# Query halves placed by DMA, feed-forward sums formed during the mixer, weights held over two halves, and low halves moved from GpSimd to VectorE

## The chip, the cores and the metric

The kernel runs on one core of a Trainium2 chip. The metric is the device time of one execution in microseconds (us), lower is better. The engines are TensorE (PE; its weight loads are PEld), VectorE (DVE), ScalarE (ACT), GpSimd (POOL) and SyncE (SP), which issues the DMAs.

## The reference

One step of a two-layer encoder over 1024 prompt frames and 32 sample frames, 1056 columns in all, width 1024. Layer A is an mLSTM mixer, layer B a sliding-window attention of 16 query heads on 2 key heads with sinks and a linear bias. Each has an output product, a residual with a layer norm, a SwiGLU feed-forward block of inner width 2816, and again a residual with a norm:

```python
def layer_norm(x, g, b):
    mu = jnp.mean(xf, -1, keepdims=True)
    var = jnp.mean(jnp.square(xf - mu), -1, keepdims=True)
    return (xf - mu) * lax.rsqrt(var + LN_EPS) * g + b

def swiglu(x, w_gu, w_down):
    g, u = jnp.split(x @ w_gu, 2, axis=-1)
    return (jax.nn.silu(g) * u) @ w_down

# every sub-layer: x = layer_norm(alpha * x + sublayer(x))
```

## The kernel before

**Layout.** x lies feature-major: 8 tiles of 128 features by 1056 columns, in `ACT` (float32) and in `SX` as a high and a low half. Columns are worked on in four quarters of 264 (two quarters are a half, `c`), in the attention in three groups of 384, 384 and 288.

**Products.** All matmuls keep float32 accuracy by splitting both operands: high is the operand rounded to the matmul type, low is the rest. `gemm` (L360 to L362) issues three matmuls per pair of tiles: high by high, high by low, low by high. So each operand needs a cast on ScalarE (for weights L200, for norms L468, for sums L1277) and a subtraction for the low half (L202, L474, L1274) on VectorE or GpSimd.

**Weights.** `Weights` loads units of 512 KB from HBM by SyncE (`wr`, three buffers, L159) and splits each in two parts, up to five live. A unit in `on_vector` has its low half on VectorE, else on GpSimd. A unit that has a `home` is split into other memory: the eight units of a mixer's output product are partly kept in `E`, which later holds the feed-forward's sums.

**Order of work.** The instruction order of each engine is fixed when the program is built. The main program writes products; `gemm` gives the estimated TensorE time of each to `wv.tick`, and the weaver `wv` lets side tasks, written as generators, issue their next step when their `yield` time has passed. `wv.drain` runs a task to its end.

**Mixer output and norm.** `mixer_out` computes the output product quarter by quarter; VectorE adds each tile to the residual (L1135) and forms the column sums (L600, L602). `ln_task` then runs as a side task: TensorE averages over the features (L421), VectorE centres (L426), ScalarE squares, L430 adds the squares (partly on GpSimd), L433 is the last addition, TensorE averages (L437), VectorE scales (L452), ScalarE applies gain and bias, and the result is split (cast L468, low half L474, odd pairs on GpSimd). The mixers' norms have `li` 0 and 2, the feed-forwards' 1 and 3; norm and products overlap by a quarter or more.

**Feed-forward.** The first two pairs of units of the up product (`FIRST` = 2) are computed plainly, for both halves: `up_plain`, 16 products of 24 matmuls per layer, with ScalarE's SiLU and VectorE's product L1253. The rest uses a seven-product scheme, `up_tile`, which needs four sums of pieces of x, called t1 to t4. `sums(c)` forms them while `up_plain` runs: VectorE adds or subtracts (L1287 to L1293) into buffers in `Z`, ScalarE casts (L1277), and L1274 forms the low half, on VectorE and GpSimd in turn:

```python
todo = [(o, k) for k in range(0, H, 2) for o in ("t3", "t2", "t4")] + [("t1", k) for k in range(0, H, 2)]
...
                        (nc.vector if s & 1 else nc.gpsimd).tensor_sub(d[:, 1], bufs[s % 2], d[:, 0].bitcast(F32))
```

**Queries.** `q_group(j, g)` makes one group of query columns for two heads. The score product (L1669, L1670) needs the high half of one head beside its low half on the other 64 partitions, so two ScalarE (L1580, L1581) and two VectorE instructions (L1582, L1585) write crosswise from PSUM into `Q`. Keys are copied across partitions by SyncE's DMAs (L1547, L1548, L1551). `attention` is a pipeline of scores (L1675 adds bias and takes a maximum), exponentials (L1687, L1691, L1693), transposes (L1713), their split (L1716, L1717) and the values; `ast["ready"]` counts the query groups it may use. Four groups are made ahead of the first scores, the other 20 while it runs.

Of the kernel before, what the change touches and what calls it, by code (L numbers as in the profile page):

```python
# [9 lines left out]
F32 = mybir.dt.float32  # L10
# [6 lines left out]
P = 128  # L17
D = 1024
KT = D // P
# [14 lines left out]

FIRST, TAIL = 2, 4
ALPHA = float((2 * DEPTH) ** 0.25)
LN_EPS = 1e-5
# [203 lines left out]
def kernel(ctx: ExitStack, tc: tile.TileContext, A, O):  # L241
# [46 lines left out]
    def add_ffn(layer):  # L288
        up, dn = {}, []
        for c in range(2):  # L290
            for i in range(FIRST):
                up[i, c] = [add("gu", 2 * (layer * FT + i) + k) for k in range(2)]
        for i in range(FIRST, FT):
            up[i] = add_pair("gu", 2 * (layer * FT + i))
        for b in range(TAIL):
            dn.append([add_pair("dn", 4 * (layer * TAIL + b) + 2 * j) for j in range(2)])
        dn.append([add("dnt", KT * layer + m) for m in range(KT)])
        on_vector.update((u, 1) for u in dn[TAIL])
        on_vector.update((u, f) for i in range(FIRST) for c in range(2) for u in up[i, c] for f in range(2))
        U_UP.append(up)  # L300
        U_DN.append(dn)
# [100 lines left out]
    def ln_task(z_, lps, grp, li, last, final):  # L402
# [20 lines left out]
        for s in range(n + 2):  # L423
# [25 lines left out]
        for s in range(n + 3):  # L449
# [138 lines left out]
    def norm_tail(li, run, box, final=False):  # L588
# [3 lines left out]
        for g, (cols, (c, zs)) in enumerate(QUARTERS):  # L592
# [18 lines left out]
            last = g >= 3  # L611
            tasks.append(wv.launch(ln_task(box[0].z, box[0].lnps, QUARTERS[g], li, last, final)))
        return tasks

# [436 lines left out]
    class Mixer(ExitStack):  # L1051
# [3 lines left out]
        def __init__(self, closing, us):  # L1055
# [7 lines left out]
            self.lnps = self.enter_context(pool("lnps", PSUM, side="right"))  # L1063
            for i, u in enumerate(us):
                for f in range(2):
                    W.home[u, f] = [self.E[:, h, 2 * i + f, : D // 2] for h in range(2)]

    def scratch(i, n):
# [49 lines left out]
    def mixer_out(us, li, lx, opening=None, before=None):  # L1118
# [3 lines left out]
        def run(g, cols, after):  # L1122
            if before:
                before(g)

            order = [6, 7, *range(6)] if g == 3 and not opening else list(range(KT))
            for i, m in enumerate(order):
# [8 lines left out]
                if g == 3 or u not in us[1]:  # L1136
                    W.done(u)
                if box[0]:
                    after(order, i)
# [10 lines left out]
    def ffn(layer, li, tasks, lx, final):  # L1150
# [15 lines left out]

        def natural(k0, par):
            return lambda c: SX[:, :, k0 : k0 + H, (2 * c + par) * N4 : (2 * c + par + 1) * N4]

        def extra(i):  # L1170
            return lambda c: E[:, :, H * i : H * (i + 1), c * N4 : (c + 1) * N4]

        X = {"x11": natural(0, 0), "x21": natural(H, 0), "x22": natural(H, 1), "t1": natural(0, 1)}
        extras = ("t2", "t3", "t4")
        X.update((o, extra(i)) for i, o in enumerate(extras))

# [61 lines left out]
        def up_plain(i, c):  # L1238
# [3 lines left out]
            for u in (ug, uu):  # L1242
                for par in range(2):
# [3 lines left out]
                    gemm(ps, wcols(u), x)  # L1247
                    if par:
                        W.done(u)
                    if u == ug:  # L1250
                        nc.scalar.activation(t, ps, AF.Silu)
                    else:
                        nc.vector.tensor_mul(t, t, ps)  # L1253

        plain = [False, False]
        made = []

        def sums(c):


            def x(k, par):
                return ACT[:, k : k + 2, group(2 * c + par)]

            todo = [(o, k) for k in range(0, H, 2) for o in ("t3", "t2", "t4")] + [("t1", k) for k in range(0, H, 2)]
            bufs = [Z[:, i : i + 2, c, :] for i in (7, 9)]
            while (li - 1, 3) not in squared:
                yield 0.3

            def halve(s, low):
                if 0 <= s < len(todo):  # L1270
                    o, k = todo[s]
                    d = X[o](c)[:, :, k : k + 2, :]
                    if low:
                        (nc.vector if s & 1 else nc.gpsimd).tensor_sub(d[:, 1], bufs[s % 2], d[:, 0].bitcast(F32))  # L1274
                        made.append((c, o))
                    else:
                        nc.scalar.copy(d[:, 0], bufs[s % 2])  # L1277

            for s in range(len(todo) + 2):
                halve(s - 2, True)  # L1280
                if s < len(todo):
                    o, k = todo[s]
                    while o == "t1" and not plain[c]:
                        yield 0.3
                    t, before = bufs[s % 2], bufs[(s - 1) % 2]
                    if o == "t3":
                        nc.vector.tensor_sub(t, x(k + H, 1), x(k, 1))  # L1287
                    elif o == "t2":
                        nc.vector.tensor_add(t, before, x(k, 0))
                    elif o == "t4":  # L1290
                        nc.vector.tensor_sub(t, x(k + H, 0), before)
                    else:
                        nc.vector.tensor_sub(t, x(k, 1), x(k, 0))  # L1293
                halve(s - 1, False)
                yield 2.6

# [60 lines left out]
        for t in tasks[:3]:  # L1357
            wv.drain(t)
        combs = []
# [12 lines left out]
        def summed(o):  # L1372
            for c in range(2):
                wv.drain(combs[c], lambda: o != "t1" and made.count((c, o)) == 2)
            if o == "t1":
                staging.append(wv.launch(stage(0)))

# [196 lines left out]
    def q_group(j, g):  # L1574

        t0, n = GRP[g]
        ps = project(U_QB[g > 0][j], g)
        q = Q[j, g] = new(pb, "Q", [P, 2, 384], F32R, bufs=4)
        sc = -(HD ** -0.5)
        nc.scalar.activation(q[0:64, 0, :n], ps[0:64], AF.Copy, scale=sc)  # L1580
        nc.scalar.activation(q[64:128, 1, :n], ps[64:128], AF.Copy, scale=sc)  # L1581
        nc.vector.scalar_tensor_tensor(  # L1582
            q[64:128, 0, :n], ps[0:64], sc, q[0:64, 0, :n].bitcast(F32), op0=ALU.mult, op1=ALU.subtract
        )
        nc.vector.scalar_tensor_tensor(  # L1585
            q[0:64, 1, :n], ps[64:128], sc, q[64:128, 1, :n].bitcast(F32), op0=ALU.mult, op1=ALU.subtract
        )

# [38 lines left out]
    for j in range(4):  # L1627
        q_group(j, 0)
        W.done(U_QB[0][j])
# [147 lines left out]
    def q_made():  # L1777
        yield 2.0
        ast["ready"] += 1
# [166 lines left out]
```

## Time and profile before

| quantity | value |
|---|---|
| median of 3 runs | 2261.14 us (2257.0 to 2265.25) |
| profiled execution | 2258.92 us, of which the span is 2257.1 us |
| mean granted TensorE clock | 0.994 |
| busy: PE, PEld | 2192.4 us, 2152.2 us |
| busy: DVE, ACT, POOL | 1490.2 us, 1016.2 us, 1076.8 us |

The span runs from the first to the last instruction of the profile. A busy figure is the time in which the engine executed something; TensorE's matmuls overlap, so its busy time is not a measure of how full it is of work. Layer A's mixer output ends and its feed-forward starts near 484 us, layer B's near 1534; the attention lies between 1200 and 1450.

### The profile page before, as it was taken

How to read it: one execution, taken by the hardware profiler on the slowest of the kernel's cores; microseconds unless marked ns; L12 is line 12 of the kernel's file. 1: busy time of each engine (PE TensorE's matmuls, PEld its weight loads, DVE VectorE, ACT ScalarE, POOL GpSimd, SP SyncE). 2: the span in 40 equal slices, each digit the busy share in tenths (PEclk: the TensorE clock that was granted, in tenths of full speed). 3: DMA queues.
4: the chain of work that ended last, by engine and by line, in shares of the span. 5: the costliest groups of instructions: out<-in, count | busy, mean ns of one | idle time of the engine just before them, and what ended most of it. 6: DMA issues, size and time to landing. Idle time of an engine off the chain costs nothing.

```text
span 2257.1 us, 44139 instructions
## 1 busy us (share of the span) xinstructions
PE 2192.4 (97%) x17086; PEld 2152.2 (95%) x17086; DVE 1490.2 (66%) x2850; ACT 1016.2 (45%) x2285; POOL 1076.8 (48%) x999
## 2 busy tenths in 40 slices
PE   9999999999999999999998999899999999999997
PEld 9899999998999999999997998899999999999997
DVE  4465577778566665566667789887666665466657
ACT  4443345464444444322246788656444444422124
POOL 2544331016666666544326775412666666654422
PEclk9999999999999999999999999999999999999999
DMA  4222112211434443696424211421344344397712
GB/s 148 76 51 69 53 39 94 87 48 67 163 135 143 152 149 138 233 329 230 154 77 139 79 60 44 136 74 47 115 153 149 133 148 154 126 343 249 256 50 77
DMA packets 167394, 291.52 MB, mean 129 GB/s; under 512 B 16593, under 2 KB 123145, under 8 KB 167185
## 3 DMA queue, kind: packets, MB, share of 16 engines
q1 hardware_dynamic: 162832, 284.38, 37.1%
q10 hardware_dynamic: 4352, 4.33, 0.5%
q8 instruction: 134, 2.20, 0.4%
q14 instruction: 76, 0.61, 0.1%
HBM read 203.89 MB, written 82.94 MB: 127 GB/s over the span
## 4 chain that ended last, share of the span: by engine, by line
PE 80%; DVE 8%; ACT 4%; DMA 3%; issue 3%; POOL 1%; SPq 0%; ACTq 0%; DVEq 0%; POOLq 0%
PE A L360 9%; PE A L362 9%; PE A L361 9%; PE d L360 9%; PE d L362 9%; PE d L361 9%; PE B L360 7%; PE B L361 7%; PE B L362 7%; PE T L1713 1%; DMA sx<-hs_t 1%; DVE wl L202 1%; DMA wr<-in_dn 1%; DVE ex L1274 1%; PE T L904 1%
## 5 line engine op out<-in xcount | busy, mean ns | idle before, releaser
L202 POOL TENSOR_TENSOR wl_s<-wr,wh_s 128x512 fp32r<-128x512 f32 x224 | 316.6, 1434 | 241.0 <-ACT wh_s L200 169.0
L360 PE MATMUL d<-sx,wh 128*128 128x264 f32 (+2 forms) x1068 | 341.1, 319 | 2.2 <-DVE z L1253 1.5
L362 PE MATMUL d<-sx,wl 128*128 128x264 f32 (+2 forms) x1068 | 326.5, 306 | 7.7 <-DVE wl L202 5.5
L361 PE MATMUL d<-sx,wh 128*128 128x264 f32 (+2 forms) x1068 | 325.7, 305 | 2.0 <-DVE sx L474 1.1
L200 ACT CAST wh_s<-wr 128x512 fp32r<-128x512 f32 x224 | 135.4, 617 | 317.0 <-DVE wr L177 289.1
L360 PE MATMUL A<-sx,wh_s 128*128 128x264 f32 x896 | 255.2, 285 | 2.8 <-ACT z L1338 2.8
L361 PE MATMUL A<-sx,wh_s 128*128 128x264 f32 x896 | 254.8, 284 | 0.0
L362 PE MATMUL A<-sx,wl_s 128*128 128x264 f32 x896 | 254.7, 284 | 0.0
L362 PEld LDWEIGHTS d<-sx,wl 128*128 128x128 f32 x1068 | 201.7, 189 | 10.1 <-DVE wl L202 7.1
L360 PEld LDWEIGHTS d<-sx,wh 128*128 128x128 f32 x1068 | 202.4, 189 | 6.0 <-issue 2.2
L361 PEld LDWEIGHTS d<-sx,wh 128*128 128x128 f32 x1068 | 202.5, 190 | 4.3 <-POOL sx L474 1.5
L202 POOL TENSOR_TENSOR wl_a<-wr,wh_a 128x512 fp32r<-128x512 f32 x112 | 169.1, 1516 | 51.4 <-ACT wh_a L200 49.8
L202 POOL TENSOR_TENSOR wl<-wr,wh 128x512 fp32r<-128x512 f32 (+2 forms) x75 | 100.1, 1343 | 173.9 <-ACT wh L200 151.3
L360 PE MATMUL d<-sx,ex 128*128 128x264 f32 x624 | 180.7, 290 | 0.4 <-ACT sx L390 0.2
L362 PE MATMUL d<-sx,ex 128*128 128x264 f32 x624 | 177.9, 285 | 3.1 <-DVE ex L202 2.6
L361 PE MATMUL d<-sx,ex 128*128 128x264 f32 x624 | 177.3, 284 | 0.2 <-DVE sx L391 0.2
L360 PEld LDWEIGHTS A<-sx,wh_s 128*128 128x128 f32 x896 | 169.0, 189 | 3.3 <-ACT z L1338 3.3
L362 PEld LDWEIGHTS A<-sx,wl_s 128*128 128x128 f32 x896 | 169.4, 189 | 0.0
L361 PEld LDWEIGHTS A<-sx,wh_s 128*128 128x128 f32 x896 | 169.0, 189 | 0.0
L1693 POOL TENSOR_SCALAR s<-s,st 128x256 f32<-128x256 f32 (+1 forms) x144 | 125.5, 884 | 67.4 <-DVE st L1691 54.7
L1208 POOL TENSOR_TENSOR z<-z 128x528 fp32r<-128x528 f32 x76 | 105.2, 1384 | 107.2 <-issue 55.5
L1207 ACT CAST z<-z 128x528 fp32r<-128x528 f32 x136 | 85.9, 631 | 95.9 <-DVE z L1220 46.0
(334 smaller groups left out, 7389.7 us busy)
## 6 DMA issues: line engine op xcount, KB each, us to landing
wr<-in_gu SPq DMA_DIRECT2D x96, 512.0 KB, 4.6
hs_x<-z SPq DMA_DIRECT2D x72, 528.0 KB, 2.8
hs_t<-z SPq DMA_DIRECT2D x64, 528.0 KB, 4.0
sx<-hs_x SPq DMA_DIRECT2D x112, 264.0 KB, 6.0
sx<-hs_t SPq DMA_DIRECT2D x64, 264.0 KB, 5.9
ex<-hs_t SPq DMA_DIRECT2D x64, 264.0 KB, 6.1
wr<-in_dn SPq DMA_DIRECT2D x32, 512.0 KB, 5.5
ex<-hs_x SPq DMA_DIRECT2D x32, 264.0 KB, 6.1
```

Source lines behind the costliest of these rows:

```text
L200: self.nc.scalar.copy(hi, r)
L202: eng.tensor_sub(lo, r, hi.bitcast(F32))
L360: nc.tensor.matmul(out, ah, bh, start=start and k == 0, stop=False, **kw)
L361: nc.tensor.matmul(out, ah, bl, start=False, stop=False, **kw)
L362: nc.tensor.matmul(out, al, bh, start=False, stop=stop and k == last, **kw)
L904: nc.tensor.matmul(pc[:, : 2 * (DV + 1)], keys, vt[j][:L, c], start=True, stop=True)
L1207: nc.scalar.copy(hi.bitcast(F32R), buf(s))
L1208: eng.tensor_sub(lo.bitcast(F32R), buf(s), hi)
L1274: (nc.vector if s & 1 else nc.gpsimd).tensor_sub(d[:, 1], bufs[s % 2], d[:, 0].bitcast(F32))
L1693: nc.gpsimd.tensor_scalar_mul(p[:R, h, lo:256], p[:R, h, lo:256], st[:R, 2, h : h + 1])
L1713: nc.tensor.transpose(pt[:nk, i, h, :R], p[:R, h, c : c + nk], ident[:R, :R])
```

## The change

1. **Held weights.** The plain up products visit (half, unit pair) in the order (0,0), (0,1), (1,1), (1,0). The second pair's units are kept from one half to the other: per layer two 512 KB loads, four casts and four subtractions fewer.
2. **Sums.** `sums` leaves the feed-forward and takes its buffers as arguments. The half c = 0 starts with the mixer's last quarter, in two buffers of its own (`su0`, `su1`); it waits until the output weights that lie in the place of a sum have been used (`lx.left`, with the homes handed out in another order) and, from its seventh step on, until the last quarter's squares are formed. The half c = 1 starts at the third visit. The difference that t2 and t4 use is formed apart from t3 (eight subtractions more in all). All low halves are on VectorE; 16 come from GpSimd.
3. **Norms.** In both mixers' norms the additions L430 and the low halves L474 that GpSimd had are on VectorE: 22 instructions.
4. **Queries.** One cast and one subtraction on all 128 partitions write `qh` and `ql`; after 1.0 us of TensorE time a side task issues four DMAs of 64 partitions that place them in `Q`: 24 ScalarE and 24 VectorE instructions fewer, 96 DMAs more. A group counts as ready after 4.0 instead of 2.0.

In the program as built, TensorE keeps its 16547 rows and VectorE its 2630, ScalarE and GpSimd have 24 rows fewer each, and SyncE goes from 616 to 711. In the changed kernel line numbers are shifted; one row of the lists below stands for one or (x2) more instructions.

```diff
+VISITS = [(0, i) for i in range(FIRST)] + [(1, i) for i in reversed(range(FIRST))]
...
-        for c in range(2):
-            for i in range(FIRST):
-                up[i, c] = [add("gu", 2 * (layer * FT + i) + k) for k in range(2)]
+        for c, i in VISITS:
+            held = up.get((i, 1 - c)) if i == FIRST - 1 else None
+            up[i, c] = held or [add("gu", 2 * (layer * FT + i) + k) for k in range(2)]
...
-                (nc.gpsimd if rush or not (last or s & 1) else nc.vector).tensor_add(acc, acc, sq[s - 2])
+                (nc.gpsimd if rush or li & 1 and not (last or s & 1) else nc.vector).tensor_add(acc, acc, sq[s - 2])
...
-                eng = nc.gpsimd if kk & 1 else nc.vector
+                eng = nc.gpsimd if kk & li & 1 else nc.vector
...
-            for i, u in enumerate(us):
+            for i, u in zip((0, 4, 1, 5, 2, 3), us):
...
+    def sums(lx, li, c, bufs, pause):
...
+        todo = [(o, k) for k in range(0, H, 2) for o in ("raw", "t2", "t4")]
+        todo += [(o, k) for o in ("t3", "t1") for k in range(0, H, 2)]
...
+                if low:
+                    nc.vector.tensor_sub(d[:, 1], bufs[s % 2], d[:, 0].bitcast(F32))
+                    lx.made.append((c, o))
+                else:
+                    nc.scalar.copy(d[:, 0], bufs[s % 2])
+
+        for s in range(len(todo) + 2):
+            if not c and s >= 6:
+                while (li, 3) not in squared:
+                    yield 0.3
+            halve(s - 2, True)
+            if s < len(todo):
+                o, k = todo[s]
+                while o == "t1" and not lx.plain[c]:
+                    yield 0.3
+                while not c and lx.left < {"t2": 1, "t4": 2}.get(o, 0) + k:
+                    yield 0.3
...
+            halve(s - 1, False)
+            yield pause
...
+            if g == 3:
+                lx = box[0]
...
+                bufs = [new(su, f"su{i}", [P, 2, N4])[:] for i in range(2)]
+                wv.drain(lx.norms[1])
+                lx.comb = wv.launch(sums(lx, li, 0, bufs, 2.4))
...
-        for c in range(2):
-            if c:
+        for c, i in VISITS:
+            if (c, i) == (1, FIRST - 1):
                 wv.drain(tasks[3])
-            combs.append(wv.launch(sums(c)))
-            for i in range(FIRST):
-                up_plain(i, c)
-            plain[c] = True
+                combs.append(wv.launch(sums(lx, li - 1, 1, [Z[:, i : i + 2, 1, :] for i in (7, 9)], 2.2)))
+            up_plain(i, c)
+            lx.plain[c] = (c, i) in (VISITS[FIRST - 1], VISITS[-1])
...
+        h, l = (new(pb, tag, [P, 384], F32R, bufs=2)[:, :n] for tag in ("qh", "ql"))
         sc = -(HD ** -0.5)
-        nc.scalar.activation(q[0:64, 0, :n], ps[0:64], AF.Copy, scale=sc)
-        nc.scalar.activation(q[64:128, 1, :n], ps[64:128], AF.Copy, scale=sc)
...
+        nc.scalar.activation(h, ps, AF.Copy, scale=sc)
+        nc.vector.scalar_tensor_tensor(l, ps, sc, h.bitcast(F32), op0=ALU.mult, op1=ALU.subtract)
+
+        def place():
+            yield 1.0
+            for i in range(2):
+                own, other = slice(64 * i, 64 * i + 64), slice(64 - 64 * i, 128 - 64 * i)
+                nc.sync.dma_start(q[own, i, :n].bitcast(F32), h[own].bitcast(F32))
+                nc.sync.dma_start(q[other, i, :n].bitcast(F32), l[own].bitcast(F32))
+
+        return wv.launch(place())
...
+    wv.drain(placing)
...
     def q_made():
-        yield 2.0
+        yield 4.0
```

VectorE in the last quarter of layer A's output product, from the additions of the third quarter's squares on, before (`act<-act,d` evacuates a product tile, `z` holds norm sums, `wl` are low halves of weights):

```order
L430 TENSOR_TENSOR z_4627<-z_4627 128x2x264
L202 TENSOR_TENSOR wl_0_5787<-wr_5062,wh_0_5786 128x512
L430 TENSOR_TENSOR z_4627<-z_4627 128x2x264
L1135 SCALAR_TENSOR_TENSOR act<-act,d_5773 128x264
L600 TENSOR_TENSOR z_4627<-act 128x2x264
L433 TENSOR_TENSOR z_4627<-z_4627 128x264
L1135 SCALAR_TENSOR_TENSOR act<-act,d_5810 128x264
L1135 SCALAR_TENSOR_TENSOR act<-act,d_5837 128x264
L600 TENSOR_TENSOR z_4627<-z_4627,act 128x2x264
L447 SCALAR_TENSOR_TENSOR z_4627<-ln_5850,eps_ln,z_4627 128x264
```

The same place after (`su` are the sums' new buffers, `ex` is where t2, t3 and t4 lie; L431, L434, L601, L1202 and L448 are the lines L430, L433, L600, L1135 and L447 of before):

```order
L431 TENSOR_TENSOR z_4627<-z_4627 128x2x264
L1120 TENSOR_TENSOR su_675_5673<-su_674_5672,act 128x528
L203 TENSOR_TENSOR wl_0_5794<-wr_5062,wh_0_5793 128x512
L431 TENSOR_TENSOR z_4627<-z_4627 128x2x264 x2
L1202 SCALAR_TENSOR_TENSOR act<-act,d_5779 128x264
L601 TENSOR_TENSOR z_4627<-act 128x2x264
L1122 TENSOR_TENSOR su_674_5672<-act,su_675_5673 128x528
L434 TENSOR_TENSOR z_4627<-z_4627 128x264
L1100 TENSOR_TENSOR ex_4623<-su_675_5673,ex_4623 128x2x264
L1118 TENSOR_TENSOR su_675_5673<-act 128x528
L1202 SCALAR_TENSOR_TENSOR act<-act,d_5817 128x264
L1100 TENSOR_TENSOR ex_4623<-su_674_5672,ex_4623 128x2x264
```

Between the first addition of squares and the evacuation that follows L433 or L434 stand five instructions before and ten after: four of the sums and one more addition of squares, which was GpSimd's, have come in.

SyncE at the start of the attention, before (`KH` and `KL` are the keys' halves, `wr` weights, `bt` and `sb` bias tables):

```order
L1551 DMA KH_13956<-KH_13956 64x384
L1551 DMA KL_13958<-KL_13958 64x384
L159 DMA wr_14090<-in_wkv 128x1024
L159 DMA wr_14134<-in_wkv 128x1024
L159 DMA wr_14179<-in_wqb 128x1024
L159 DMA wr_14236<-in_wqb 128x1024
L159 DMA wr_14295<-in_wqb 128x1024
```

And after (`qh` and `ql` are the new halves):

```order
L1571 DMA KH_13946<-KH_13946 64x384
L1571 DMA KL_13948<-KL_13948 64x384
L160 DMA wr_14080<-in_wkv 128x1024
L160 DMA wr_14124<-in_wkv 128x1024
L1608 DMA Q_14111<-qh_14112 64x384
L1609 DMA Q_14111<-ql_14113 64x384
L1608 DMA Q_14111<-qh_14112 64x384
L1609 DMA Q_14111<-ql_14113 64x384
L160 DMA wr_14173<-in_wqb 128x1024
L1608 DMA Q_14160<-qh_14161 64x384
L1609 DMA Q_14160<-ql_14162 64x384
```

The placing transfers stand between the weight loads, four for each query group.

More of the change, by code (lines that the diff above doesn't have):

```diff
@@ L1165, in bank @@
             return new(px.pool[tag], tag, [P, 2, 512], bufs=2)[:, :, :N4]
[L1167 to L1173, printed above, removed]
+        X = seven(E)
         extras = ("t2", "t3", "t4")
-        X.update((o, extra(i)) for i, o in enumerate(extras))
         def tiles(t):
@@ L1253, in up_plain @@
                         nc.vector.tensor_mul(t, t, ps)
[L1255 to L1295, printed above, removed]
         tail = []
@@ L1373, in summed @@
             for c in range(2):
-                wv.drain(combs[c], lambda: o != "t1" and made.count((c, o)) == 2)
+                wv.drain(combs[c], lambda: o != "t1" and lx.made.count((c, o)) == 2)
             if o == "t1":
+                lx.sums.close()
                 staging.append(wv.launch(stage(0)))
@@ L1627 @@
     for j in range(4):
[L1628 removed]
+        placing = q_group(j, 0)
         W.done(U_QB[0][j])
```

41 lines of the change are left out of this document (33 added, 8 removed).

## The prediction

> **What bounds the kernel now.** I read the page's totals first, then the windows around the two feed-forward starts, the waits there, and the groups by shape.
>
> ```profile
> span 2257.1 us, 44139 instructions
> PE 2192.4 (97%) x17086; PEld 2152.2 (95%) x17086; DVE 1490.2 (66%) x2850; ACT 1016.2 (45%) x2285; POOL 1076.8 (48%) x999
> ```
>
> TensorE is busy for 97% of the span and the change leaves its 16547 matmul and transpose rows in the program as they are, so a gain can only come from TensorE's pauses. No other engine is near full on average, but an average over stages hides the stage that matters. The windows show it (columns: us, then busy us and count of PE, PEld, DVE, ACT, POOL, then granted clock, DMA share, GB/s):
>
> ```profile
> 470.00:480.00 10.00, 10.00 (x83) 9.93 (x83) 5.51 (x12) 2.36 (x5) 1.29 (x1) 1.00 0.01 4
> 510.00:520.00 10.00, 8.48 (x63) 7.63 (x62) 9.97 (x11) 5.61 (x11) 6.07 (x5) 1.00 0.16 54
> 520.00:530.00 10.00, 8.04 (x64) 7.64 (x63) 9.90 (x12) 4.88 (x9) 5.18 (x3) 1.00 0.15 52
> 530.00:540.00 10.00, 9.11 (x73) 8.72 (x72) 9.97 (x11) 3.95 (x9) 6.60 (x4) 1.00 0.16 52
> 540.00:550.00 10.00, 8.92 (x71) 8.49 (x71) 6.16 (x8) 5.50 (x10) 7.51 (x5) 1.00 0.15 54
> 550.00:560.00 10.00, 10.00 (x84) 10.00 (x84) 6.96 (x10) 2.81 (x5) 5.27 (x5) 1.00 0.37 135
> 1560.00:1570.00 10.00, 8.43 (x63) 7.58 (x62) 9.96 (x12) 6.01 (x12) 6.07 (x4) 1.00 0.17 52
> 1570.00:1580.00 10.00, 8.05 (x64) 7.66 (x64) 9.93 (x11) 4.49 (x9) 5.57 (x4) 1.00 0.17 55
> 1580.00:1590.00 10.00, 8.97 (x72) 8.55 (x70) 9.93 (x12) 4.34 (x9) 6.59 (x4) 1.00 0.17 54
> 1590.00:1600.00 10.00, 9.05 (x70) 8.66 (x71) 6.54 (x9) 5.50 (x10) 7.13 (x5) 1.00 0.15 54
> ```
>
> An undisturbed stretch at full clock (550 to 560) holds 84 matmuls in 10 us, so 0.119 us each. From 510 to 550 there are 63 + 64 + 73 + 71 = 271 instead of 336: 65 missing, 7.7 us. The second layer has 63 + 64 + 72 + 70 = 269, 67 missing, 8.0 us. In three of the four windows of each layer VectorE is full (9.90 to 9.97 of 10) while it completes only 11 or 12 instructions. Who waits for it, from 505 to 600 (line waited for: total us, times, longest):
>
> ```profile
> PE d L362 <- DVE wl L202: 2.8, 3, 1.2
> ```
>
> VectorE is full because each of its instructions there is long. The groups from 505 to 546, with one VectorE group from 476 to 482, where GpSimd stood nearly still:
>
> ```profile
> L1274 DVE TENSOR_TENSOR ex<-z,ex 128x528 fp32r<-128x528 f32 x6 | 8.7, 1446 | 0.0
> L1253 DVE TENSOR_TENSOR z<-z,d 128x264 f32<-128x264 f32 x6 | 2.4, 416 | 0.0
> L1274 POOL TENSOR_TENSOR ex<-z,ex 128x528 fp32r<-128x528 f32 x5 | 8.9, 1778 | 6.0 <-ACT ex L1277 6.0
> L452 DVE TENSOR_TENSOR act<-act,z 128x528 f32<-128x528 f32 x4 | 2.6, 701 | 0.0
> ```
>
> The same size (128x528, two operands in SBUF) lasts 701 ns when GpSimd is quiet and 1446 ns while GpSimd subtracts alongside. L1253, with one operand in PSUM, keeps its 416 ns.
>
> **The change, part by part.** All counts below are of the built order; big means 512 or 528 columns, small 264.
>
> *Sums early, low halves and norm shares on VectorE, held weights (both layers).* I count two stages. The last quarter of the mixer's output product holds 194 matmuls; at 83 per 10 us that is 23.4 us. VectorE has 19 big + 12 small instructions there before and 29 + 12 after, GpSimd 3 before and none after. At 0.70 and 0.42 us VectorE's work grows from 18.3 to 25.3 us: it is now fuller than the stage is long. Back to back it is a little better:
>
> ```profile
> 479.09 1.32 DVE L452 TENSOR_TENSOR act<-act,z 128x528 f32<-128x528 f32 x2
> 480.34 0.42 DVE L1135 SCALAR_TENSOR_TENSOR act<-act,d 128x264 f32<-128x264 f32 x1
> ```
>
> Two big ones take 1.25 us to the next start, 0.63 each, and by that, with 0.40 taken for a small one, the stage holds 23.1 us of work. So VectorE is between 0.3 us under and 1.9 us over, and loses the slack that it had. What waits for it there are the norms' sums that TensorE multiplies:
>
> ```profile
> 473.03 0.42 DVE L433 TENSOR_TENSOR z<-z 128x264 f32<-128x264 f32 x1
> 474.90 0.61 PE L437 MATMUL ln<-z,onesm 128*128 128x264 f32 x2
> 484.33 1.44 DVE L602 TENSOR_TENSOR z<-z 128x264 f32<-128x264 f32 x1
> 486.98 0.60 PE L421 MATMUL ln<-z,onesm 128*128 128x264 f32 x2
> ```
>
> The slack is 474.90 − 473.45 = 1.45 us and 486.98 − 485.77 = 1.2 us. It roughly covers the overrun; I charge 0.8 us a layer for what sticks out, with 0 and 1.9 as bounds.
>
> The plain products behind it hold 386 matmuls, 46.0 us at 84 per 10 us. VectorE goes from 47 + 12 instructions to 51 + 12, GpSimd from 14 to 3, ScalarE's casts from 39 to 33. At the quiet price VectorE needs 51 x 0.70 + 12 x 0.42 = 40.7 us, which fits into 46.0 with 5.3 to spare; before, at up to 1.4 us each, 47 + 12 did not. The spare time also takes the backlog from the quarter before. The held weights are in these counts: 4 subtractions and 4 casts fewer per layer, and two 512 KB loads, which hide anyway at a DMA share of 0.16. The eight extra subtractions (t3's difference is formed anew) are in them too. The three remaining GpSimd splits can lengthen three VectorE instructions by about 0.75 us each: 2.2 us, inside the spare 5.3. I leave 1.0 us a layer of the old stall, with 0 and 2.2 as bounds.
>
> Together: 7.7 + 8.0 − 2 x (0.8 + 1.0) = 12.1 us gained.
>
> *Queries.* Per group two ScalarE and two VectorE instructions on half the partitions become one each on all 128, and four 96 KB transfers put the halves in place.
>
> ```profile
> PE psS L1669 <- DVE st L1675: 5.6, 1, 5.6
> PE T L1713 <- DVE lo L1717: 7.1, 5, 2.3
> L1581 ACT ACTIVATE Q<-d x24: 406/486/489, 1208.7 to 1409.7; 64x384 fp32r<-64x384 f32 x16, 64x288 fp32r<-64x288 f32 x8
> L1585 DVE SCALAR_TENSOR_TENSOR Q<-d,Q x24: 459/559/561, 1211.8 to 1410.8; 64x384 fp32r<-64x384 f32 x16, 64x288 fp32r<-64x288 f32 x8
> ```
>
> Time per instruction goes with columns, not partitions, so 24 x 0.49 us leave ScalarE and 24 x 0.56 us VectorE. Most of it lies beside other work. One longest wait (5.6 us, from 1200 to 1300) ends behind this chain, and loses the 0.5 us of L1581. Two of the five waits for L1717 (1355 to 1450) come right behind query instructions: 0.5 each. Less backlog on VectorE may give another 1.0. That is 2.5 us, between 0.5 and 6.
>
> The transfers cost where a query is used soon after it is made. The tight place is the first query of the second wave:
>
> ```profile
> 1264.55 0.48 ACT L1580 ACTIVATE Q<-d 64x384 fp32r<-64x384 f32 x1 [0.25 <-PE d L362]
> 1267.23 0.28 PE L1669 MATMUL psS<-KH,Q 128*128 128x256 f32 x1
> 1255.64 0.47 SPq L1547 DMA_DIRECT2D KH<-KH  x1
> 1256.15 0.59 SPq L1548 DMA_DIRECT2D KH<-KH  x1
> KH<-KH SPq DMA_DIRECT2D x6, 96.0 KB, 4.1
> KL<-KL SPq DMA_DIRECT2D x6, 96.0 KB, 2.2
> ```
>
> The keys are already spread by the same kind of transfer, so there is a price. Four issues 0.5 to 0.6 us apart and a landing of 2.2 to 4.1 us put a query in place 4.2 to 6.5 us after its low half. The first score came 2.7 us after ScalarE's start; the new order puts it about 20 matmuls, 2.4 us, later, since readiness is now told after 4.0 instead of 2.0. I take 1.0 us in all, between 0 and 5. Behind the waiting issues on SyncE stand weight loads and the bias tables, which have several us until they are used.
>
> The Trainium skill's page "DMA: Bandwidth & Descriptors" ("Rules for kernel authors") speaks against this part: two transfers to disjoint partition halves run one after the other, and one over 128 partitions is to be used. Worked out from the keys' rows, an estimate by that rule is 4 x 2.2 = 8.8 us from first issue to last landing, 2 to 4 us later than I take; at the two or three tight queries the sum would be some 5 us worse. The rows show issues that overlap their landings; that a second half waits for a first, no row shows.
>
> Queries net: 2.5 − 1.0 = 1.5 us gained. **Sum:** 12.1 + 1.5 = 13.6. The profiled execution took 2258.92 us (span 2257.1), so 2245.3; it lies 2.2 below the median of 2261.14, and on that scale I forecast 2247 (2247.5 rounded down).
>
> **Rivals.**
>
> *A, VectorE's backlog becomes TensorE's wait in the mixer.* If the added 25.3 − 18.3 = 7.0 us do not slip into gaps, the evacuations L1135 come late and TensorE runs out of PSUM banks. For it: after the change the stage has no slack on VectorE. Against it: the window 470 to 480 has VectorE at 5.51 of 10. The cost per layer lies between 1.9 and 7.0; at 4.5 instead of 0.8 the time is 2247 + 2 x 3.7 = 2254.4. A pause may also cost clock:
>
> ```profile
> PE A L360 <- ACT z L1338: 1.8, 1, 1.8
> 580.00:590.00 10.00, 10.00 (x73) 10.00 (x73) 8.03 (x8) 3.49 (x7) 5.21 (x4) 0.85 0.14 54
> ```
>
> Behind a single 1.8 us wait the granted clock was 0.85 for 10 us, 1.5 us lost. With one such stretch a layer, A's upper end is 2247 + 2 x (7.0 − 0.8 + 1.5) = 2262. The Trainium skill's page "TensorE: Matmul & The Clock Gate" ("Why this matters for your kernels") has the clock fall only after gaps above about 3 us, by which such a wait would cost itself alone; this row differs from it, and I go by the row.
>
> *B, slower: queries land too late throughout.* All 20 groups after the first wave may be asked for before their four transfers land. It ends slower once the mean shortfall reaches (2267.9 − 2247 + 1.0)/20 = 1.1 us; at 1.5 us the time is 2276. For it: 6.5 us at worst against the 2.7 of the row above. Against it: the last query is made at 1409.7 and scores run on to 1442.9, so the lead grows as the stage goes on:
>
> ```profile
> L1669 PE MATMUL psS<-KH,Q x144: 221/282/582, 1221.8 to 1442.9; 128*128 128x256 f32 x112, 128*128 128x128 f32 x16, 128*32 128x160 f32 x16
> ```
>
> *C, more is gained.* The feed-forward starts close completely (3.6 us more) and half of the remaining (5.6 − 0.5) + (7.1 − 1.0) = 11.2 us of attention waits goes: 2238.
>
> *D, the change does not empty GpSimd.* If its weight splits are pulled ahead into the plain products, VectorE stays slow and about half of 12.1 remains: 2253. The built order has 3 of them there, which speaks against it.
>
> **How the numbers follow.** Chances: forecast 0.63, A 0.14, B 0.07, C 0.12, D 0.04. A difference of 0.3%, 6.8 us, is about what a measurement can tell: faster is under 2254.4, slower over 2267.9. Faster: 0.61 of the forecast, C, four tenths of A, most of D: 0.81. Same: the rest of these, 0.12. Slower: 0.07. The range 2236 to 2257 holds the forecast with its bounds, C and most of A, and leaves out B and the outer ends, some 0.17.
>
> **What would show it.** Right: in the windows from 510 to 550 and 1560 to 1600 (some us earlier now) 80 or more matmuls per 10 us, GpSimd under 2 of 10, and the low halves on VectorE near 0.70 us. Wrong: those windows stay near 65 (D); 75 or fewer from 462 to 486, with waits for L1135 or the norms' sums (A); first scores that wait for Q's transfers in most groups, with VectorE idle (B).

## The result, and the profile after

| | before | after |
|---|---|---|
| median of 4 runs | 2259.72 us (2257.0 to 2265.25) | 2245.39 us (2242.24 to 2246.22) |
| profiled execution, its span | 2258.92, 2257.1 us | 2244.99, 2242.9 us |

The ratio is 0.9926, 95% interval [0.9911, 0.9941]: 14.3 us faster by the medians, against a forecast of 2247 in the range 2236 to 2257.

The totals of the page after:

```profile
PE 2187.7 (98%) x17086; PEld 2151.6 (96%) x17086; DVE 1472.7 (66%) x2864; ACT 999.6 (45%) x2253; POOL 1018.3 (45%) x961
```

The windows of the changed kernel at the two feed-forward starts (columns as before: us, then busy us and count of PE, PEld, DVE, ACT, POOL, granted clock, DMA share, GB/s):

```profile
460.00:480.00 20.00, 20.00 (x163) 19.74 (x162) 19.11 (x35) 10.64 (x19) 0.00 (x0) 1.00 0.16 54
480.00:500.00 20.00, 19.46 (x158) 19.15 (x157) 17.36 (x30) 14.17 (x26) 0.00 (x0) 1.00 0.14 40
510.00:520.00 10.00, 10.00 (x85) 10.00 (x84) 8.81 (x15) 6.91 (x14) 0.00 (x0) 1.00 0.06 14
520.00:530.00 10.00, 10.00 (x85) 10.00 (x84) 9.90 (x14) 4.57 (x9) 2.98 (x3) 1.00 0.27 93
530.00:540.00 10.00, 9.76 (x79) 9.46 (x79) 8.11 (x12) 4.46 (x8) 5.23 (x4) 1.00 0.01 2
540.00:550.00 10.00, 10.00 (x85) 10.00 (x84) 2.72 (x5) 3.93 (x7) 6.63 (x6) 1.00 0.44 140
1560.00:1570.00 10.00, 10.00 (x84) 10.00 (x84) 9.86 (x15) 4.59 (x10) 1.77 (x2) 1.00 0.36 107
1570.00:1580.00 10.00, 9.76 (x79) 9.45 (x78) 8.22 (x13) 4.28 (x9) 5.26 (x4) 1.00 0.00 0
1580.00:1590.00 10.00, 10.00 (x85) 10.00 (x84) 3.83 (x5) 3.50 (x7) 6.68 (x6) 1.00 0.36 107
1590.00:1600.00 10.00, 10.00 (x85) 10.00 (x84) 7.47 (x9) 4.29 (x9) 5.28 (x5) 1.00 0.27 110
```

From 510 to 550 there are now 334 matmuls instead of 271, from 1560 to 1600 333 instead of 269. VectorE still reaches 9.90 of 10, but does 14 instructions in such a window and not 11 or 12. What it cost stands in two places: 158 matmuls from 480 to 500, and 79 from 530 to 540. Before, the quarter ahead of the feed-forward was undisturbed:

```profile
460.00:480.00 20.00, 20.00 (x164) 19.86 (x163) 15.03 (x26) 9.19 (x17) 4.32 (x3) 1.00 0.16 54
480.00:500.00 20.00, 20.00 (x164) 19.87 (x163) 14.54 (x24) 14.93 (x26) 2.81 (x2) 1.00 0.15 54
```

TensorE's waits from 470 to 545 in the changed kernel are short ones (line waited for: total us, times, longest):

```profile
PE ln L422 <- DVE z L603: 0.5, 1, 0.5
PE A L363 <- POOL wl_s L203: 0.2, 1, 0.2
```

The groups of VectorE from 490 to 535, by shape, show the price of an instruction:

```profile
L1100 DVE TENSOR_TENSOR ex<-z,ex 128x528 fp32r<-128x528 f32 x6 | 5.3, 886 | 0.0
L475 DVE TENSOR_TENSOR sx<-act,sx 128x528 fp32r<-128x528 f32 x4 | 2.8, 705 | 1.2 <-ACT sx L469 1.2
L1100 DVE TENSOR_TENSOR ex<-su,ex 128x528 fp32r<-128x528 f32 x4 | 2.8, 701 | 0.0
```

With GpSimd silent the low halves last 701 ns, as the quiet row of before said. The first group mixes them with one that met GpSimd.

To compare stretches, the traces can be laid on each other: TensorE has the same 17086 records in each, so the time between two records of the same number is the same work. Three stretches serve for all kernels: the feed-forward starts of layer A (numbers 3250 to 4000) and layer B (11250 to 12050), and the attention (8750 to 11000). The median is that of a kernel's runs, the stretches are of one profiled run each. What lies outside them is the same work in all and varied by up to 5 us between profiles, by 1.7 us between the two of the changed kernel. The starts agree within 0.02 us between these two, the attention only within 1.1.

| kernel | median us | start A | start B | attention |
|---|---|---|---|---|
| before | 2259.72 | 99.78 | 105.85 | 330.97 |
| changed | 2245.39 | 93.31 | 99.20 | 327.88 |
| changed again | 2244.51 | 93.33 | 99.18 | 328.94 |
| VectorE only | 2254.48 | 96.36 | 102.45 | 330.69 |
| early, halves on GpSimd | 2254.76 | 98.18 | 104.03 | 328.56 |
| idle GpSimd work | 2262.07 | 106.42 | 103.25 | 330.45 |
| queries only | 2259.36 | 99.77 | 105.87 | 327.52 |
| weights not held | 2249.02 | 95.37 | 101.45 | 328.34 |
| ready after 2.0 | 2249.89 | 93.28 | 99.20 | 333.56 |
| first tile on VectorE | 2242.86 | 92.65 | 98.59 | 330.14 |
| norms on GpSimd | 2244.27 | 93.07 | 98.96 | 328.78 |
| low halves on GpSimd | 2252.25 | 96.64 | 104.07 | 328.61 |
| first tile, ready after 5.0 | 2242.02 | 92.71 | 98.57 | 325.62 |
| the three edits together | 2240.21 | 92.44 | 98.38 | 325.69 |

By these profiles the change gained 6.5 and 6.7 us at the starts and 2.0 to 3.1 us in the attention.

### The profile page after: what moved, and what is told of

Read it like the earlier page. It is cut to its first block, busy times and chain, and to the rows that moved or that the text cites. A ratio compares the mean times of both kernels' runs of the same rounds, so it can differ in the third digit from the quotient of the medians.

```text
span 2242.9 us, 44249 instructions
## 1 busy us (share of the span) xinstructions
PE 2187.7 (98%) x17086; PEld 2151.6 (96%) x17086; DVE 1472.7 (66%) x2864; ACT 999.6 (45%) x2253; POOL 1018.3 (45%) x961
## 4 chain that ended last, share of the span: by engine, by line
PE 80%; DVE 8%; ACT 4%; DMA 3%; issue 3%; POOL 1%; SPq 0%; ACTq 0%; DVEq 0%; POOLq 0%
PE A L361 9%; PE A L363 9%; PE A L362 9%; PE d L361 8%; PE d L363 8%; PE d L362 8%; PE B L361 7%; PE B L362 7%; PE B L363 7%; PE T L1737 1%; DMA wr<-in_dn 1%; ACT act L463 1%; PE T L906 1%; PE O L1752 1%; DVE wl L203 1%
```

## The experiments

Each kernel was timed beside the kernel before on the same chip, whose median there lay between 2262.18 and 2263.11.

**VectorE only.** The kernel before with one part of the change:

```diff
-                (nc.gpsimd if rush or not (last or s & 1) else nc.vector).tensor_add(acc, acc, sq[s - 2])
+                (nc.gpsimd if rush or li & 1 and not (last or s & 1) else nc.vector).tensor_add(acc, acc, sq[s - 2])
-                eng = nc.gpsimd if kk & 1 else nc.vector
+                eng = nc.gpsimd if kk & li & 1 else nc.vector
-                        (nc.vector if s & 1 else nc.gpsimd).tensor_sub(d[:, 1], bufs[s % 2], d[:, 0].bitcast(F32))
+                        nc.vector.tensor_sub(d[:, 1], bufs[s % 2], d[:, 0].bitcast(F32))
```

> The kernel before with one part of the change: all low halves of the sums and GpSimd's share of both mixers' norms on VectorE, but the sums still start with the feed-forward, the weights are not held and the queries are as before. Theory T (GpSimd's reads are what lengthens VectorE's instructions): the plain products hold 58 big and 12 small VectorE instructions, 58 x 0.70 + 12 x 0.42 = 45.6 us against 46.0 us of matmuls, so most of the stall goes: 3 to 7 us a layer, 2246 to 2254, most likely 2250. Rival R (the work has to be begun earlier): VectorE stays full, under 2 us a layer gained or a loss, 2256 or more.

Measured 2254.48, ratio 0.9969 [0.9957, 0.9981], 7.7 us faster; 3.4 us at each start. R's size is out, though VectorE does stay full, as R had it. T is at the low end of its gain a layer, and the time lies just outside its range. Two of this kernel's windows show why:

```profile
510.00:520.00 10.00, 8.03 (x64) 7.61 (x63) 9.86 (x18) 6.83 (x15) 0.00 (x0) 1.00 0.18 54
520.00:530.00 10.00, 9.12 (x75) 8.91 (x74) 9.83 (x15) 6.38 (x14) 1.28 (x1) 1.00 0.14 52
```

VectorE does 18 instructions in 10 us instead of 11 and is still full, and TensorE still lacks 20 matmuls from 510 to 520. Quiet instructions alone give about half of the 6.5 and 6.7 us; what is left here is that too much is to be done at once.

**Early, halves on GpSimd.** The changed kernel with the three lines above as they were before.

> The changed kernel without that part: early sums, held weights and placed queries stay, but half of the sums' low halves and the norms' share are on GpSimd again. In the plain products GpSimd has 13 instructions instead of 3, VectorE 41 big instead of 51. T: each GpSimd instruction lengthens a VectorE instruction by about 0.75 us, 10 x 0.75 = 7.5 us, against 10 x 0.70 = 7.0 us that leave VectorE: no relief, and PE loses 1 to 5 us a layer: 2247 to 2255. R: the early start alone closes the stall: 2243 to 2247.

Measured 2254.76, ratio 0.9971 [0.9958, 0.9984], in T's range; R's 2247 is out. Of the 6.5 and 6.7 us at the starts, 1.6 and 1.8 are left. Taken one by one the two parts give 3.4 + 1.6 and 3.4 + 1.8, less than together. But part of the loss here is clock: TensorE waits once in each layer, 2.6 and 2.7 us, for a copy of ScalarE, and the granted clock falls behind both waits. One of the windows:

```profile
540.00:550.00 10.00, 7.43 (x47) 7.40 (x48) 3.50 (x4) 4.86 (x9) 8.02 (x6) 0.83 0.24 66
```

The kernel with the low halves on GpSimd, further on, has the same wait in both layers and the fall in one alone; by it the fall costs some 1.5 us. With that taken off, the parts give 3.4 + 3.1 and 3.4 + 3.3: as far as single profiles tell, they add. The wait itself isn't T's reason alone, as the same kernel shows.

**Idle GpSimd work.** The changed kernel, with work for GpSimd that nobody waits for, into a buffer `idle` that is set to zero once a layer:

```diff
                 if low:
                     nc.vector.tensor_sub(d[:, 1], bufs[s % 2], d[:, 0].bitcast(F32))
+                    if lx.li:
+                        nc.gpsimd.tensor_copy(lx.idle, d[:, 1].bitcast(F32))
+                    else:
+                        nc.gpsimd.tensor_sub(lx.idle, lx.idle, d[:, 1].bitcast(F32))
```

> The changed kernel, with one more GpSimd instruction behind each low half of the sums, 16 a layer, whose result nobody reads: in layer A a subtraction of two operands in SBUF, in layer B a copy of one. The plain products then hold 14 GpSimd instructions, as many as in the kernel before. T: in layer A VectorE's 128x528 instructions beside them go from 0.70 to 1.2 us or more, VectorE needs 11 x 0.75 = 8.3 us more with 5.3 to spare, and PE loses 2 to 7 us there. R: nobody waits for these instructions, so nothing changes (under 0.5 us). Layer B tells whether a GpSimd instruction of one operand does the same: the same loss if any read by GpSimd counts, about half if it is the operands.

Measured 2262.07, ratio 1.0007 [0.9997, 1.0016]: work without a reader takes the whole gain away. Layer A loses 13.1 us at its start, layer B 4.1. VectorE's and GpSimd's groups of layer A, 500 to 550:

```profile
L1100 DVE TENSOR_TENSOR ex<-z,ex 128x528 fp32r<-128x528 f32 x6 | 9.5, 1582 | 0.0
L1104 POOL TENSOR_TENSOR idle<-idle,ex 128x528 f32<-128x528 f32 x10 | 17.7, 1766 | 36.9 <-DVE ex L1100 36.2 <-PE B L362 0.7
L1322 DVE TENSOR_TENSOR z<-z,d 128x264 f32<-128x264 f32 x6 | 2.4, 418 | 0.0
```

And of layer B, 1550 to 1600, with the copies:

```profile
L1100 DVE TENSOR_TENSOR ex<-z,ex 128x528 fp32r<-128x528 f32 x6 | 6.7, 1110 | 0.0
L1102 POOL COPY idle<-ex 128x528 f32<-128x528 f32 x10 | 10.9, 1086 | 38.1 <-DVE ex L1100 38.1
```

The same low half lasts 886 ns in the changed kernel, 1110 beside copies and 1582 beside subtractions, while the instruction with a PSUM operand keeps 418. No other path of the added work is seen: from 500 to 560 TensorE's only wait for GpSimd is the one of 0.2 us that the changed kernel has too, and VectorE has none. That is the mechanism, alone. The rivalry of T and R is settled, but T's size was far off in layer A (2 to 7). The windows there say where the rest went:

```profile
530.00:540.00 10.00, 7.49 (x60) 7.11 (x58) 9.93 (x8) 4.24 (x9) 7.88 (x6) 1.00 0.17 52
540.00:550.00 10.00, 4.40 (x28) 3.98 (x29) 9.39 (x12) 3.57 (x7) 7.14 (x5) 0.86 0.01 2
550.00:560.00 10.00, 10.00 (x69) 10.00 (x68) 2.47 (x5) 2.28 (x5) 7.46 (x6) 0.79 0.34 105
```

TensorE waited 4.9 us in one piece for a copy of ScalarE, and the clock was then granted at 0.86 and 0.79. ScalarE in turn stood in its queue behind a weight cast that waited for VectorE:

```profile
547.06 1.14 ACT L201 CAST wh_s<-wr 128x512 fp32r<-128x512 f32 x2 [4.35 <-DVE wr L178]
548.11 0.59 ACT L1348 COPY z<-A 128x528 f32<-128x528 f32 x1
548.75 0.59 PE L361 MATMUL A<-ex,wh_s 128*128 128x264 f32 x1 [4.86 <-ACT z L1348]
```

L178 is a difference of weights on VectorE for the next product: the backlog reaches TensorE by way of ScalarE's queue. In layer B the wait is 2.5 us, and the clock fell behind it too (0.83 from 1590 to 1600), so neither loss is a pause alone.

**Queries only.** The kernel before with the changed `q_group`, the task that places, and the 4.0 in `q_made`.

> The kernel before with the placed queries alone. T (the parts add): the two traces differ by 3.1 us across the attention, so 2256.6, between 2255 and 2258.5, and the feed-forward starts as before. Rival: the difference across the attention comes with the other parts (the attention starts 5.5 us earlier and its pauses meet the clock otherwise): within 1 us of 2259.7.

Measured 2259.36 against 2262.18, ratio 0.999 [0.9977, 1.0003]: 2.8 us, which the interval doesn't tell from none. The starts are as before (99.77 and 105.87), and in this profile, the fastest of the ten runs, the attention is 3.5 us shorter. Over all kernels of the table it is less clear: in the nine profiles with placed queries that are ready after 4.0 the attention takes 327.5 to 330.5 us, in the two without them 331.0 and 330.7. All nine are shorter, by 2.0 us on average. So the part seems to add to the others; a gain of 3 us isn't shown.

**Weights not held.**

```diff
-            held = up.get((i, 1 - c)) if i == FIRST - 1 else None
-            up[i, c] = held or [add("gu", 2 * (layer * FT + i) + k) for k in range(2)]
+            up[i, c] = [add("gu", 2 * (layer * FT + i) + k) for k in range(2)]
-                    if par and (c or i < FIRST - 1):
+                    if par:
```

> The changed kernel, but the second pair's units are loaded and split anew for the second half (two loads, four casts and four VectorE subtractions more per layer). T (VectorE's fullness sets the stall): the plain products hold 55 big and 12 small VectorE instructions, 43.5 us of 46.0, so little is lost: 0 to 1 us a layer, 2245 to 2248. Rival H (the loads or casts were in the way): 2 us a layer or more, over 2249.

Measured 2249.02, ratio 0.9938 [0.9925, 0.9952], beside 0.9919 [0.9905, 0.9933] of the changed kernel: 4.5 us lost, 2.0 and 2.3 of it at the starts. T's size is out, and H's numbers came true. What was in the way? One window:

```profile
510.00:520.00 10.00, 9.45 (x73) 8.84 (x72) 9.84 (x18) 7.04 (x15) 0.00 (x0) 1.00 0.18 54
```

VectorE is full here, with 18 instructions, and TensorE waits 0.6 us in this window for a low half of the norm (L474). GpSimd is silent and DMA is at 0.18. The spare time of 2.5 us, worked out over 46 us, isn't there in these 10. But fullness is not where it begins. From 498 to 512 the changed kernel casts and splits no weight. This kernel does so twice, and VectorE waits for the second cast; the norm's first low half follows (start, length, in brackets the idle time before):

```profile
509.31 0.69 DVE L203 TENSOR_TENSOR wl<-wr,wh 128x512 fp32r<-128x512 f32 x1 [1.60 <-ACT wh L201]
511.16 0.70 DVE L474 TENSOR_TENSOR sx<-act,sx 128x528 fp32r<-128x528 f32 x1
```

In the changed kernel that low half is its line L475:

```profile
508.32 0.70 DVE L475 TENSOR_TENSOR sx<-act,sx 128x528 fp32r<-128x528 f32 x1
```

It comes 2.8 us later here: 1.6 us are the wait for the cast, the rest the two subtractions. So in this window of layer A H's casts are in the way at least as much as T's fullness. What the other losses are made of was not separated. VectorE and ScalarE wait for no load there.

**Ready after 2.0.** In `q_made`, `yield 2.0` instead of 4.0.

> The changed kernel with a query group counted as ready after 2.0 instead of 4.0, so that its scores follow its four transfers up to 2 us sooner. T (only the first groups of the second wave are tight): 0 to 4 us lost, all of it near the second wave's start, 2245 to 2249. Rival B (the transfers' landing is what every group waits for): up to 2 us in each of 20 groups, 2255 or more.

Measured 2249.89, ratio 0.9941 [0.9928, 0.9955]: 5.4 us lost, a little over T's bound and short of B's. TensorE's waits from 1170 to 1300:

```profile
PE psS L1693 <- DMA Q<-qh: 3.7, 1, 3.7
PE psS L1693 <- DMA Q<-ql: 3.1, 2, 2.6
```

Three scores wait, 6.8 us together, all between 1264 and 1277, and none after 1300: the transfers of two or three of the 20 groups come late. With 4.0, the first profile of the changed kernel has one such wait from 1240 to 1300, its second none:

```profile
PE psS L1693 <- DMA Q<-qh: 1.1, 1, 1.1
```

**First tile on VectorE.**

```diff
+        on_vector.update((up[FIRST], f) for f in ("a1", "a2", "b2", "s2"))
```

> The changed kernel with the first four low halves of the first seven-product tile's weights on VectorE instead of GpSimd, in both layers. The plain products then hold no GpSimd instruction and 54 big ones of VectorE, 54 x 0.70 + 12 x 0.42 = 42.8 us of 46.0. T: the three VectorE instructions beside GpSimd go from 1.8 back to 0.7 us and the wait for the low half of s2 goes: 0.5 to 1 us a layer gained, 2243.5 to 2245. Rival: the subtractions stand in VectorE's queue ahead of the last sums and the tile starts later: 1 to 3 us a layer lost.

Measured 2242.86, ratio 0.9913 [0.9899, 0.9927], and 2244.51 for the changed kernel beside it. The intervals overlap, so by the totals the 1.6 us are not clear. At the starts it gains 0.7 and 0.6 us, as T had it, and the window that lacked 5 matmuls lacks none:

```profile
530.00:540.00 10.00, 10.00 (x85) 10.00 (x84) 8.08 (x13) 3.32 (x6) 2.37 (x2) 1.00 0.01 2
```

**Changed again.**

> The changed kernel itself, on the same chip as the three others, to compare them with: 2245.4, within 2.

Measured 2244.51, ratio 0.9919 [0.9905, 0.9933], as expected.

**Norms on GpSimd, and low halves on GpSimd.** Each gives back one of the two kinds: the lines of `ln_task`, or the line of `sums`.

> The changed kernel with GpSimd's share of both mixers' norms given back to GpSimd: 3 instructions in the mixer's last quarter (VectorE 26 big instead of 29) and 4 in the plain products (VectorE 47 instead of 51, GpSimd 7 instead of 3). T (VectorE's price beside GpSimd): the quarter gives 3 x 0.70 back but has 3 x 0.75 more, and so has the plain part: 0 to 2 us a layer lost, 2245 to 2249. Rival A (the quarter's fullness costs): the 0.9 us that each layer's feed-forward start lost behind the full quarter come back, 2243 to 2244.

> The changed kernel with the sums' low halves on VectorE and GpSimd in turn again, the norms' share stays on VectorE: 8 GpSimd instructions in the plain products instead of 3, 45 big ones of VectorE instead of 51. T: with the kernel that gave both back (2254.8) and the one that gives the norms back (up to 2249) it must make up the rest: 2 to 4 us a layer lost, 2249 to 2253. R (only the early start counts): 2244 to 2246.

With the norms on GpSimd: 2244.27, ratio 0.9923 [0.9904, 0.9942], the same as changed; 0.2 us shorter at each start. This part of the change brought no gain that can be seen. T's loss is out; rival A's direction is right and its size too large. The pause behind the quarter goes, but a smaller one comes in before it, 321 matmuls in all from 460 to 500 as in the changed kernel:

```profile
460.00:480.00 20.00, 19.79 (x160) 19.45 (x159) 19.53 (x30) 11.05 (x20) 4.45 (x3) 1.00 0.16 54
480.00:500.00 20.00, 19.99 (x161) 19.68 (x161) 17.81 (x30) 13.87 (x26) 2.84 (x2) 1.00 0.13 37
```

With the low halves on GpSimd: 2252.25, ratio 0.9956 [0.994, 0.9972], 7.7 us over the changed kernel and in T's range, 3.3 and 4.9 at the starts, some 1.5 of the 4.9 by the clock (last section). So it is the sums' low halves that count. But the view of VectorE isn't the expected one. A group of it from 500 to 546 (the last column is idle time before it and who ended it):

```profile
L1118 DVE TENSOR_TENSOR z<-act 128x528 f32<-128x528 f32 x4 | 2.8, 706 | 2.6 <-POOL ex L1100 2.5
```

The timeline, a row each of VectorE, ScalarE and TensorE (start, length, in brackets the idle time before):

```profile
535.31 1.78 DVE L1124 TENSOR_TENSOR z<-act 128x528 f32<-128x528 f32 x1 [1.60 <-POOL ex L1100]
539.96 1.14 ACT L201 CAST wh_s<-wr 128x512 fp32r<-128x512 f32 x2 [2.15 <-DVE wr L178]
541.65 0.39 PE L361 MATMUL A<-ex,wh_s 128*128 128x264 f32 x1 [2.64 <-ACT z L1341]
```

The window of these rows:

```profile
530.00:540.00 10.00, 9.01 (x75) 8.80 (x73) 7.93 (x12) 3.16 (x7) 4.24 (x4) 1.00 0.01 3
```

VectorE is not full, 7.93 of 10. It waits: the sums have two buffers, the next sum may not overwrite one until GpSimd has formed its low half, and GpSimd has other work ahead of it, such as a weight's low half that itself waited 4.75 us for TensorE, to 527.4. Behind VectorE's waiting instruction stand the weight differences, behind those ScalarE's casts and the copy L1341 that TensorE wants. So there are two mechanisms: in the kernel before, VectorE's group of low halves has 0.0 us of idle time, and the length of its instructions is what shows; once the work is spread, the round trip to GpSimd comes in. Lengthened instructions are still there (1.78 us in the first row), so the shares of the two in this kernel are not separated. Low halves on VectorE remove both.

**First tile, ready after 5.0.**

> The changed kernel with the first tile's low halves on VectorE and a query group ready after 5.0 instead of 4.0. T: the one wait of 1.1 us for a placed query goes, the rest stays: 0.5 to 1.5 us faster than with 4.0, 2241 to 2242.5. Rival: the scores move on by one step in the order and pauses elsewhere in the attention grow: 2243 to 2247.

Measured 2242.02, ratio 0.9908 [0.9892, 0.9923]. No query waits for its transfers in this profile, and its attention is the shortest (325.62); by the totals the step from 4.0 is not clear. Three of the nine profiles with 4.0 have no such wait either, so the shorter attention (325.69 in the next kernel, 327.5 or more with 4.0) is not explained by it alone.

**The three edits together.**

> The changed kernel with three edits together: the first tile's low halves on VectorE, queries ready after 5.0, and GpSimd's share of both mixers' norms given back to GpSimd. If the parts add, each layer's feed-forward start loses neither the 0.5 us behind the full quarter nor the 0.6 us of the first tile, and no query waits for its transfers: 1 us less than without the norms' edit, 2240 to 2242. If the quarter's GpSimd work only moves the wait, no different from 2242.

Measured 2240.21 (2236.46 to 2246.04), ratio 0.9909 [0.9891, 0.9926]: the lowest median of all, though its interval overlaps that of the changed kernel and its runs spread over 10 us, so it isn't told from 2242 either. By the stretches it is 0.9 and 0.8 us shorter than the changed kernel at the starts and 2.2 to 3.3 in the attention.

## Why the prediction was right, and where it wasn't

**The ceiling and its cause.** Of the 15.7 us at the starts 6.47 + 6.65 = 13.1 us came, where 12.1 were forecast. VectorE's lengthened instructions are a cause, as predicted: idle GpSimd work alone brings a stall back. They are not the whole cause. Taking them away alone gave 3.4 us a layer; the rest came with the earlier start and the held weights.

**The charge for the full quarter**, 0.8 us a layer: 164 + 164 matmuls before and 163 + 158 after from 460 to 500, 7 x 0.119 = 0.8 us in layer A. **What is left of the stall**, 1.0 us: five or six matmuls in one window, 0.6 to 0.7 us, and the experiment with the first tile shows that the three GpSimd splits are its cause. Rival A did not happen; only its small part, the charge. Of the signs named, the matmuls came (84 or 85 a window, 79 in one of each layer). GpSimd under 2 of 10 came in only two of the eight windows: its weight splits for the seven-product tiles now fall into the others.

**The spare 5.3 us** is the step that doesn't hold. It was averaged over the 46 us of the plain products. By the same average 2.5 us are spare without the held weights, and yet 4.5 us are lost: VectorE is at 9.84 of 10 from 510 to 520, and its free time lies where it doesn't help, before (5.49 of 10 from 500 to 510, a cast's wait among it) and after 540 (3.44). The sum came out because the held weights were part of the counts.

**The norms' share** was counted as a help in making GpSimd silent. By the run it is none here: with the norms back on GpSimd the starts are 0.2 us shorter, and the pause behind the quarter is only split in two.

**Low halves.** The prediction knew one reason for moving them, the shared price; the second, VectorE's wait for GpSimd behind two buffers, it did not have. It shows only once the work is spread.

**Queries.** Forecast 2.5 − 1.0 = 1.5 us net, measured 2.0 on average over the nine profiles, between 0.4 and 3.3, against the mean of the two without. The price of the transfers was 0 to 1.3 us in these profiles, 1.1 in the first of the changed kernel, at the place that was named. Rival B is refuted: even with 2 us less only three scores waited. In the first profile of the changed kernel, the four transfers of a group land 4.0 to 4.7 us after the first issue where the trace has the last one's landing (one issued 2.27 us after the first landed at 4.66, another 1.93 and 3.96); the latest landing of any, a third one's, is at 5.95. The 8.8 us worked out from the rule on two halves (the Trainium skill, "DMA: Bandwidth & Descriptors", "Rules for kernel authors") are not seen: a later transfer is issued before an earlier one has landed, and the landing times don't add. Whether the bytes of two halves move one after the other these landings don't show.

**Rivals C and D** did not happen either. **The total.** The forecast of 2247 lay 1.6 us above the median, and 1.4 of that is the scale: it was set on a median before of 2261.14, and with the fourth run that is 2259.72. The gain was forecast as 13.6 and is 14.3. That it agrees so well is in part luck: in the first profile the three stretches gained 16.2 us, and 2.0 us were lost again outside them.

## What to carry to other kernels

When an engine is full only in one stage, look first at the mean time of its instructions there against the same shape elsewhere: here their length had doubled, and taking the neighbour's work over was cheaper than sharing it. Then look at when the work comes: normal length alone gave half. An average of free time over a stage doesn't pay for what is added at its start; count in windows as short as the queue in front of the waiting engine. Follow a wait through every in-order queue: TensorE's wait named ScalarE, and the cause was two engines behind.

## What the runs showed of the hardware

A pause of TensorE of about 2 us may or may not cost clock. In layer A, between 570 and 585 us, each kernel waits once for a copy of ScalarE. The window from 570 to 580 in the first profile of the changed kernel, where the wait was 1.9 us:

```profile
570.00:580.00 10.00, 8.07 (x54) 7.86 (x53) 7.88 (x9) 3.97 (x8) 5.11 (x4) 0.83 0.27 110
```

In the kernel with the three edits together, where it was 2.2 us:

```profile
570.00:580.00 10.00, 8.38 (x69) 8.39 (x70) 8.48 (x9) 3.92 (x8) 5.71 (x4) 1.00 0.27 109
```

Over all kernels the clock fell there behind waits of 1.8 (before), 1.9, 1.8 and 2.0 us and stayed at 1.00 behind 1.3, 1.6, 1.7, 1.9, 2.0 and 2.2 us. Fifteen matmuls hang on it, 1.8 us, as much as the pause itself, so a difference of 2 us between single profiles can be this alone. "TensorE: Matmul & The Clock Gate" of the Trainium skill ("Why this matters for your kernels") puts the bound at about 3 us; these runs show falls below it. What decides between them stays open; the length of the wait alone doesn't. One run shows it best, the low halves on GpSimd. TensorE waits 2.64 us for the copy L1341 in both layers, to 541.7 and to 1587.1. Layer A and layer B behind it:

```profile
540.00:550.00 10.00, 8.35 (x67) 8.32 (x68) 4.67 (x7) 4.83 (x9) 8.03 (x6) 1.00 0.31 89
550.00:560.00 10.00, 10.00 (x85) 10.00 (x84) 5.54 (x10) 4.30 (x8) 4.65 (x4) 1.00 0.32 127
1580.00:1590.00 10.00, 7.36 (x54) 7.11 (x53) 7.21 (x8) 4.38 (x8) 5.87 (x5) 0.91 0.03 5
1590.00:1600.00 10.00, 10.00 (x78) 10.00 (x78) 2.63 (x4) 3.15 (x6) 6.34 (x6) 0.92 0.32 105
```

The same 100 matmuls around the wait (numbers 3800 to 3900 and 11800 to 11900) take 15.15 us in layer A and 16.67 in layer B: the fall costs 1.5 us.

The price of GpSimd's company on VectorE depends on what GpSimd does: 1582 ns beside subtractions of two operands in SBUF (1766 ns each), 1110 beside copies of one (1086 ns each), for an instruction of 701 ns. The two differ in operation, operands and length, and which of these counts was not separated. One that reads PSUM kept its time (418 ns).
